# Splitting weights by whole chunks, table functions in program order, and the first norm's factor on another engine

## The chip, the cores and the metric

The kernel runs on one core of one Trainium2 chip. The metric is the device time of one execution in microseconds, as the median of several runs.

## The reference

A trunk of four layers works on 256 tokens of width 1024 in float32. Every layer is a token mixer and an MLP, each behind an RMS norm and added to the residual:

```python
for i in range(DEPTH):                       # DEPTH = 4
    kind, j = i % 3, i // 3                  # mixers a, b, c, a
    h = _rmsnorm(x, norm_mix_g[i])
    x = x + mixer[kind](h, ...)
    x = x + jnp.square(jax.nn.relu(_rmsnorm(x, norm_mlp_g[i]) @ mlp_w1[i])) @ mlp_w2[i]
return _rmsnorm(x, final_norm_g)

def _rglru_mixer(h, ...):                    # mixer a: layers 0 and 3
    gate, xr = jnp.split(h @ w_in, 2, axis=-1)          # 1024 -> 2 x 1280
    gate = jax.nn.gelu(gate)
    xr = _causal_dwconv(xr, conv_w) + conv_b            # 4 taps
    r, ig = sigmoid(block_diag(xr, gate_a_w) + gate_a_b), sigmoid(block_diag(xr, gate_x_w) + gate_x_b)
    log_a = -8 * r * softplus(-lam)
    a, u = exp(log_a), sqrt(-expm1(2 * log_a)) * (ig * xr)
    hs = scan(h_t = a_t * h_(t-1) + u_t)                # over 256 tokens
    return (hs * gate) @ w_out                          # 1280 -> 1024
```

Mixer b (layer 1) is a gated MLP whose gate is mixed over the tokens of a chunk of 128, mixer c (layer 2) a gated short convolution. The MLPs go from 1024 to 4096 and back.

## The kernel before, in words

**Layout.** Channels lie on the 128 partitions and tokens on the free axis. A tile of two channel blocks, 128x512, is a *pair*; the 1280 recurrent channels are five pairs, 0 to 4.

**Precision.** Every product is made of three float32r matmuls (`mm3`, L162, issued at L164): each operand is a high part plus a low part, and high x high, high x low and low x high are added in PSUM. The activations are split by `split` (L326: ACT casts at L329, DVE subtracts at L330) or by `prep` (L190).

**Weights.** They come as chunks of 128x2048 float32 (1 MB) in the order of their use, in two loads of 512 KB each on SP's queue (L132). ACT casts the raw half to the high part (`whi`, L135) and DVE subtracts for the low part (`wlo`, L136). The raw halves have twelve slots of 128x1024 (`rawp`, L94), the split chunks five buffers each (L95, L96). `next_chunk` (L143) keeps four split chunks ahead of the one in use. The gate weights of mixer a are block-diagonal and used whole in float32, without a split (`whole`, L114): three chunks for each of two groups, held in raw slots until TensorE has read them. A chunk's load is issued once its slot is free: after the split of the earlier tenant, or after the gate matmuls that read it.

**Order.** TensorE (PE) runs in program order (L76). The other engines' order is set by the scheduler when the kernel is built, by priorities: the weight work is put 150 places later than it stands (`LATER`), the recurrence and the norm's factor 100 earlier (`SOON`). Each engine then runs its instructions strictly in that written order.

**Mixer a** (L404 to L518) runs by `LRU_ORDER`: the convolved branch in three products (4, 2 and 4 channel blocks; weight chunks 0 and 1, 2, and 3 and 4), the gelu gate of pairs 0 and 1 (chunks 5 and 6), the first group of gate matmuls (L451; 20 instructions), the recurrence of pairs 0 and 1, the second group, the recurrence of pairs 2, 3 and 4, the gelu gate of pair 2 (one chunk) and of pairs 3 and 4 (two), then the out-projection, one chunk of 48 matmuls a pair. A pair's out-projection needs `hs` times gate (L498) as high and low part.

**The recurrence** (`recur`, L457) makes of a pair: two tanh and two exp on ACT (L467), four ops on DVE (L469 to L473), a square root on ACT (L475), then on DVE L476, L477, the affine step `q = -0.5 q - 1` (L478) and two scans (L481). ACT holds one set of table functions at a time; tanh and exp, gelu, and sqrt each call for a table load where the set changes.

**The norm.** The squares' sum goes through PE (`first`, L242, into L245), a factor 1/sqrt by ACT (L228) and 14 small ops on POOL (L229 to L235, L251, L252), DVE builds two diagonal matrices (L257), and PE spreads the factor over the partitions (`second`, L260, L263); ACT copies it out (L267). `hooks` (L502) says behind which matmuls PE does either: in layer 0 the first behind the first branch product, the second in the third.

## Time and profile before

| | |
|---|---|
| median of 3 runs | 1093.49 us (1093.09 to 1093.8) |
| the profiled execution | 1093.35 us, its span 1091.6 us |
| mean granted TensorE clock | 0.993 |
| busy: PE, DVE, ACT, POOL | 98%, 67%, 56%, 3% |
| matmuls | 9078 |
| HBM read | 202.51 MB, 186 GB/s over the span |
| table loads on ACT | 19, of 1.28 us |

Busy shares are means over stages that have different limits, so the stages are read one by one. A row of the timeline gives start, duration, engine, line, operation, output and inputs, and the number of instructions merged into it; a bracket at its end gives the idle time before it and what ended that. A row of a window gives the stretch, its length, the busy time and number of instructions of PE, of its weight loads (PEld), of DVE, ACT and POOL, then the granted clock of PE, the DMA share and GB/s. A row of a group gives the count, then busy time and mean ns of one.

### The profile page before, as it was taken

The page shows a single profiled execution, that of the slowest core. Times are in us where ns is not written, and L with a number is a line of the kernel's source. Part 1 is how long each engine was busy: PE and PEld are TensorE (multiplying, and loading weights), DVE is VectorE, ACT ScalarE, POOL GpSimd, SP SyncE. Part 2 cuts the span into 40 slices and gives each one's busy share as a digit, 9 for nine tenths or more (in the row PEclk, how much of TensorE's full clock was granted, in tenths as well). Part 3 has the DMA queues.
Part 4 walks back from the last instruction along what each step waited for, and adds up shares of the span by engine and source line. Part 5 has one row for each costly group of instructions (what it writes and reads, how often), then busy time and mean ns, then how long its engine had stood idle before and what let it go on. Part 6 is the DMA issues. An engine that isn't in the chain of part 4 may idle for free.

```text
span 1091.6 us, 21721 instructions
## 1 busy us (share of the span) xinstructions
PE 1066.9 (98%) x9078; PEld 1055.7 (97%) x9078; DVE 734.8 (67%) x991; ACT 609.7 (56%) x847; POOL 36.1 (3%) x139
## 2 busy tenths in 40 slices
PE   7998999999999999999999999999999999999996
PEld 7997999999999999999999999999999989999995
DVE  6989866555748766555777775556579698655553
ACT  6699655444655555444644555445457896544442
POOL 1000100000020100000010010000010001000000
PEclk9998999999999999999999999999999999999998
DMA  9754765555466565555466466555545447555301
GB/s 329 265 210 135 246 230 189 197 194 195 159 208 207 182 211 192 195 193 194 157 211 208 159 219 204 195 194 190 197 151 198 155 133 249 202 199 195 124 1 39
DMA packets 58802, 204.97 MB, mean 188 GB/s; under 512 B 6480, under 2 KB 8656, under 8 KB 58704
## 3 DMA queue, kind: packets, MB, share of 16 engines
q1 hardware_dynamic: 58288, 203.19, 55.0%
q8 instruction: 71, 1.16, 0.4%
q10 hardware_dynamic: 416, 0.39, 0.1%
q14 instruction: 27, 0.22, 0.1%
HBM read 202.51 MB, written 1.05 MB: 186 GB/s over the span
## 4 chain that ended last, share of the span: by engine, by line
PE 84%; DVE 7%; ACT 5%; DMA 2%; issue 1%; POOL 1%; SPq 0%; DVEq 0%; ACTq 0%; POOLq 0%
PE ps L164 80%; DMA raw<-weights 2%; PE ps L542 2%; DVE wlo L136 2%; DVE xc L481 1%; ACT q L467 1%; PE ps L451 1%; DVE xc L429 1%; ACT th L467 1%; ACT whi L135 1%; DVE ig L477 1%; ACT rg L455 0%; ACT L475 0%; ACT ig L455 0%; POOL rc L229 0%
## 5 line engine op out<-in xcount | busy, mean ns | idle before, releaser
L136 DVE TENSOR_TENSOR wlo<-raw,whi 128x1024 fp32r<-128x1024 f32 (+1 forms) x376 | 443.6, 1211 | 225.9 <-ACT whi L135 225.9
L135 ACT CAST whi<-raw 128x1024 fp32r<-128x1024 f32 (+1 forms) x376 | 376.1, 1038 | 325.2 <-issue 290.9
L164 PE MATMUL ps<-xs,whi 128*128 128x256 f32 x3200 | 550.7, 277 | 6.6 <-ACT whi L135 6.5
L164 PEld LDWEIGHTS ps<-xs,whi 128*128 128x128 f32 x3200 | 484.4, 188 | 7.0 <-ACT whi L135 6.5
L164 PE MATMUL ps<-xs,wlo 128*128 128x256 f32 x1600 | 442.9, 277 | 0.0
L164 PE MATMUL ps<-hi,whi 128*128 128x256 f32 x1312 | 363.7, 277 | 4.6 <-ACT hi L329 4.6
L164 PE MATMUL ps<-lo,whi 128*128 128x256 f32 x1312 | 364.1, 278 | 1.8 <-DVE lo L330 1.6
L164 PE MATMUL ps<-hi,wlo 128*128 128x256 f32 x1312 | 363.5, 277 | 0.7 <-DVE wlo L136 0.7
L164 PEld LDWEIGHTS ps<-xs,wlo 128*128 128x128 f32 x1600 | 301.3, 188 | 0.2 <-DVE wlo L136 0.2
L164 PEld LDWEIGHTS ps<-hi,whi 128*128 128x128 f32 x1312 | 247.6, 189 | 4.8 <-ACT hi L329 4.8
L164 PEld LDWEIGHTS ps<-lo,whi 128*128 128x128 f32 x1312 | 247.5, 189 | 2.9 <-DVE lo L330 2.5
L164 PEld LDWEIGHTS ps<-hi,wlo 128*128 128x128 f32 x1312 | 247.6, 189 | 0.9 <-DVE wlo L136 0.9
L344 DVE SCALAR_TENSOR_TENSOR u<-ps,rs 128x512 f32<-128x512 f32 x64 | 44.0, 687 | 33.2 <-PE ps L164 33.2
L346 ACT ACTIVATE hi<-u 128x512 fp32r<-128x512 f32 x64 | 40.3, 630 | 35.1 <-DVE u L344 35.1
L348 DVE TENSOR_TENSOR lo<-hsq,hi 128x512 fp32r<-128x512 f32 x64 | 44.1, 689 | 14.8 <-ACT hsq L347 12.2
L195 ACT ACTIVATE xs<-x,cst 128x256 fp32r<-128x256 f32 x64 | 29.4, 501 | 30.2 <-DVE x L315 29.1
L347 ACT ACTIVATE hsq<-u 128x512 f32<-128x512 f32 x64 | 39.4, 615 | 0.0
L196 DVE SCALAR_TENSOR_TENSOR xs<-x,cst,xs 128x256 fp32r<-128x256 f32 x64 | 28.8, 482 | 8.7 <-ACT xs L195 8.7
L229 POOL TENSOR_SCALAR rc<-rc 128x2 int32<-128x2 int32 x9 | 9.9, 1096 | 723.4 <-ACT rc L228 723.4
L257 DVE TENSOR_SCALAR diag<-eye,rc 128x128 fp32r<-128x128 f32 x36 | 8.1, 286 | 30.9 <-POOL rc L251 30.9
L451 PE MATMUL ps<-xc,raw 128*128 128x256 f32 x112 | 28.4, 379 | 0.0
L429 DVE SCALAR_TENSOR_TENSOR xc<-xr,cst,xc 128x255 f32<-128x255 f32 (+2 forms) x60 | 25.4, 481 | 0.8 <-ACT xc L425 0.6
(111 smaller groups left out, 476.0 us busy)
## 6 DMA issues: line engine op xcount, KB each, us to landing
raw<-weights SPq DMA_DIRECT2D x377, 512.0 KB, 4.7
raw<-weights SPq DMA_DIRECT2D x12, 256.0 KB, 4.5
x<-xT SPq DMA_DIRECT2D x8, 128.0 KB, 4.3
sb<-sbias SPq DMA_DIRECT2D x2, 256.0 KB, 4.9
outT<-o SPq DMA_DIRECT2D x2, 256.0 KB, 2.3
outT<-o ACTq DMA_DIRECT2D x1, 256.0 KB, 2.3
cst<-consts SPq DMA_DIRECT2D x1, 132.0 KB, 2.2
outT<-o ACTq DMA_DIRECT2D x1, 128.0 KB, 1.8
```

The source lines that it names most:

```text
L135: nc.scalar.copy(out=hi[:, s], in_=raw[:, e])
L136: nc.vector.tensor_tensor(out=lo[:, s], in0=raw[:, e], in1=hi.bitcast(F32)[:, s], op=SUB)
L164: nc.tensor.matmul(ps, a, b, start=start and n == 0, stop=stop and n == 2, skip_group_check=True)
L195: nc.scalar.activation(xs[:, hi], x, AF.Copy, scale=g)
L196: nc.vector.scalar_tensor_tensor(out=xs[:, lo], in0=x, scalar=g, in1=xs.bitcast(F32)[:, hi], op0=MULT, op1=SUB)
L344: nc.vector.scalar_tensor_tensor(out=u, in0=ps, scalar=0.0, in1=both(scale.row), op0=MAX, op1=MULT)
L346: nc.scalar.activation(hi, u, AF.Square)
L347: nc.scalar.activation(sq, u, AF.Square)
L348: nc.vector.tensor_tensor(out=lo, in0=sq, in1=hi.bitcast(F32), op=SUB)
L429: nc.vector.scalar_tensor_tensor(out=conv[:, j, d:], in0=raw[:, j, :T - d], scalar=tap(i), in1=conv[:, j, d:], op0=MULT, op1=ADD)
L451: nc.tensor.matmul(ps[:, e, :], w[:, at % 8, :], x, start=n == 0, stop=n == 1)
L467: nc.scalar.activation(dst[:, j, :], rg[i][:, j, :], fn, scale=lam[:, c:c + 1], bias=lam[:, c:c + 1])
```

## The change

Four edits. A raw slot is now a whole chunk (six slots of 128x2048 in the place of twelve of 128x1024), and a chunk is cast by one instruction and split by one, after both of its loads; chunks 0 and 1 are still done by 512 columns, and 2 and 3 by 1024 (`AHEAD` is 4). The half-width gate chunks take a whole slot each. In mixer a the table functions are chained in program order by a dependence without a semaphore (`function`), and the square roots of all pairs of a call come ahead of the DVE ops behind them. The affine step moves from DVE to ACT. In layer 0 the norm's factor is made on DVE, and its `second` moves into the second branch product; the start-up computation of `lam2` and `lam4` moves behind the first sums.

```diff
-    rawp = pool("rawp", 12 * 4096, 0, bufs=12)
+    rawp = pool("rawp", 6 * CHUNK * 4, 0, bufs=6)
...
-    def fetch(i, step=1024):
+    def fetch(i, step=CHUNK):
         n = widths[i]
         if i in whole:
-            raw = rawp.tile([P, 1024], F32, name="raw", tag="raw")
+            raw = rawp.tile([P, CHUNK], F32, name="raw", tag="raw")[:, :CHUNK // 2]
...
+        raw = rawp.tile([P, CHUNK], F32, name="raw", tag="raw")
+
+        def load(s):
+            for c in range(s.start, s.stop, 1024):
+                e = slice(c, min(c + 1024, s.stop))
+                nc.sync.dma_start(out=raw[:, e], in_=weights[i, :, e])
+
+        def part(s):
+            nc.scalar.copy(out=hi[:, s], in_=raw[:, s])
+            nc.vector.tensor_tensor(out=lo[:, s], in0=raw[:, s], in1=hi.bitcast(F32)[:, s], op=SUB)
+
+        return [(lambda s=s: load(s), lambda s=s: part(s))
+                for s in (slice(c, min(c + step, n)) for c in range(0, n, step))]
...
-                for load, part in fetch(asked[0]):
+                for load, part in fetch(asked[0], 1024 if asked[0] < AHEAD else CHUNK):
...
-    def rsqrt(ss, table=False):
+    def rsqrt(ss, table=False, eng=nc.gpsimd):
...
-        nc.gpsimd.tensor_scalar(out=y.bitcast(I32), in0=v.bitcast(I32), scalar1=-0.5, scalar2=float(RSQRT_SEED),
+        eng.tensor_scalar(out=y.bitcast(I32), in0=v.bitcast(I32), scalar1=-0.5, scalar2=float(RSQRT_SEED),
...
+    last_fn = []
+
+    def function(*args, **kw):
+        ins = nc.scalar.activation(*args, **kw).ins
+        if last_fn:
+            tc.add_manual_dep(ins, last_fn.pop().name,
+                              mybir.DependencyInfo(mybir.DependencyClass.NoSync, mybir.DependencyReason.DATA),
+                              reason="tables")
+        last_fn.append(ins)
...
             for i in pairs:
-                nc.scalar.activation(th[i], th[i], AF.Sqrt)
+                function(th[i], th[i], AF.Sqrt)
+            for i in pairs:
...
-                nc.vector.tensor_scalar(out=qs[i], in0=qs[i], scalar1=-0.5, scalar2=-1.0, op0=MULT, op1=ADD)
+                nc.scalar.activation(qs[i], qs[i], AF.Copy, scale=-0.5, bias=-1.0)
...
-        hooks = [{7: scale.first}, {}, {0: scale.second}] if layer == 0 else [{6: scale.first}, {6: scale.second}, {}]
+        hooks = ([{7: lambda: scale.first(eng=nc.vector)}, {5: scale.second}, {}] if layer == 0 else
+                 [{6: scale.first}, {6: scale.second}, {}])
...
-    softplus_lambda()
     for k in range(KD):
...
         sumsq(i)
+    softplus_lambda()
```

The tanh and exp of the gates and of the recurrence and the gelu of `gated` go through `function` too; that edit is left out above.

**What it moves.** The order in which the instructions are written, engine by engine, is shown at three places. Line numbers are each kernel's own: the cast is L135 before and L132 now, the split L136 and L133, the loads L132 (gate weights L116) and L129 (L116).

DVE, layer 0, the first weights behind chunks 0 and 1. Before, `whi_238` is chunk 2 (of raw halves 240 and 241), `whi_248` chunk 3:

```order
L136 TENSOR_TENSOR wlo_239<-raw_240,whi_238 128x1024
L136 TENSOR_TENSOR wlo_239<-raw_241,whi_238 128x1024
L136 TENSOR_TENSOR wlo_249<-raw_250,whi_248 128x1024
L257 TENSOR_SCALAR diag_398<-eye_101,rc2_394 128x128 x2
L257 TENSOR_SCALAR diag_401<-eye_101,rc2_395 128x128 x2
L136 TENSOR_TENSOR wlo_249<-raw_251,whi_248 128x1024
L136 TENSOR_TENSOR wlo_259<-raw_260,whi_258 128x1024
```

Now, behind the first halves of chunk 2 (`whi_236`) and chunk 3 (`whi_245`), from the end of the norm's factor on (`whi_254` is chunk 4, `whi_309` chunk 5):

```order
L248 CAST rc2_384<-rc_368 128x2
L249 TENSOR_TENSOR rc2_385<-rc_368,rc2_384 128x2
L254 TENSOR_SCALAR diag_388<-eye_101,rc2_384 128x128 x2
L254 TENSOR_SCALAR diag_391<-eye_101,rc2_385 128x128 x2
L133 TENSOR_TENSOR wlo_255<-raw_256,whi_254 128x2048
L133 TENSOR_TENSOR wlo_246<-raw_247,whi_245 128x1024
L133 TENSOR_TENSOR wlo_237<-raw_238,whi_236 128x1024
L133 TENSOR_TENSOR wlo_310<-raw_311,whi_309 128x2048
```

The second half of chunk 2 (`wlo_237`) has moved behind the factor, all of chunk 4 and the second half of chunk 3; SP's loads and ACT's casts of these stand in the same new order.

SP's queue, layer 0, around the loads of the gate weights (L116), with the semaphores that each waits for. Before:

```order
L116 DMA raw_423<-weights 128x1024 [waits DMAHW7_49,DVE_49]
L116 DMA raw_425<-weights 128x512 [waits DMAHW0_49,DVE_49]
L132 DMA raw_479<-weights 128x1024 [waits DMAHW1_49,DVE_49]
L132 DMA raw_480<-weights 128x1024 [waits DMAHW2_49,DVE_49]
L132 DMA raw_542<-weights 128x1024 [waits DMAHW3_49,DVE_49]
L132 DMA raw_543<-weights 128x1024 [waits DMAHW4_49,DVE_49]
```

Now:

```order
L116 DMA raw_410<-weights 128x1024 [waits DMAHW7_49,DMAHW0_49,DVE_49]
L129 DMA raw_397<-weights 128x1024
L116 DMA raw_412<-weights 128x512 [waits DMAHW7_49,DMAHW1_49,DVE_49]
L129 DMA raw_511<-weights 128x1024 [waits DMAHW2_49,PE_49]
L129 DMA raw_511<-weights 128x1024
L129 DMA raw_566<-weights 128x1024 [waits DMAHW3_49,PE_49]
L129 DMA raw_566<-weights 128x1024 [waits DMAHW4_49]
```

The chunks behind the gate weights (479 and 542 before, 511 and 566 now) waited for DVE's splits; now they wait for PE, which has to have read the gate weights in their slots.

DVE, layer 0, in the recurrence of pairs 0 and 1, from L477 (now L484) on. Before:

```order
L477 TENSOR_TENSOR ig_232<-ig_232,th_834 128x512
L481 SCALAR_TENSOR_TENSOR xc_600<-q_825,ig_231 128x256 x2
L478 TENSOR_SCALAR q_835<-q_835 128x512
L473 SCALAR_TENSOR_TENSOR ig_233<-ig_233,xc_627 128x512
L481 SCALAR_TENSOR_TENSOR xc_613<-q_835,ig_232 128x256 x2
L498 TENSOR_TENSOR xc_600<-xc_600,gate_783 128x512
L498 TENSOR_TENSOR xc_613<-xc_613,gate_786 128x512
L136 TENSOR_TENSOR wlo_726<-raw_728,whi_725 128x1024
L330 TENSOR_TENSOR lo_858<-xc_600,hi_857 128x512
L136 TENSOR_TENSOR wlo_951<-raw_952,whi_950 128x1024
L330 TENSOR_TENSOR lo_863<-xc_613,hi_862 128x512
L136 TENSOR_TENSOR wlo_951<-raw_953,whi_950 128x1024
```

Now:

```order
L484 TENSOR_TENSOR ig_230<-ig_230,th_809 128x512
L133 TENSOR_TENSOR wlo_565<-raw_566,whi_564 128x2048
L488 SCALAR_TENSOR_TENSOR xc_469<-q_800,ig_229 128x256 x2
L488 SCALAR_TENSOR_TENSOR xc_482<-q_810,ig_230 128x256 x2
L479 SCALAR_TENSOR_TENSOR ig_231<-ig_231,xc_496 128x512
L505 TENSOR_TENSOR xc_469<-xc_469,gate_758 128x512
L505 TENSOR_TENSOR xc_482<-xc_482,gate_761 128x512
L133 TENSOR_TENSOR wlo_649<-raw_650,whi_648 128x2048
L327 TENSOR_TENSOR lo_833<-xc_469,hi_832 128x512
L133 TENSOR_TENSOR wlo_704<-raw_705,whi_703 128x2048
L327 TENSOR_TENSOR lo_838<-xc_482,hi_837 128x512
L133 TENSOR_TENSOR wlo_926<-raw_927,whi_925 128x2048
```

The affine step (L478) is gone from DVE, and the splits in the stretch are others: three of the twelve rows before are splits of half a chunk, four of the twelve now are splits of a whole one. Two more whole splits (`wlo_991` and `wlo_1046`) follow ahead of the low part of pair 2 (`lo_985`).

More of the change, by code (lines that the diff above doesn't have):

```diff
@@ L123, in fetch @@
         ready[i] = (hi, lo)
-        steps = []
-        for c0 in range(0, n, 1024):
-            c1 = min(c0 + 1024, n)
-            raw = rawp.tile([P, 1024], F32, name="raw", tag="raw")
-            for c in range(c0, c1, step):
-                steps.append((raw, slice(c - c0, min(c + step, c1) - c0), slice(c, min(c + step, c1))))
-        def load(raw, e, s):
-            nc.sync.dma_start(out=raw[:, e], in_=weights[i, :, s])
-        def part(raw, e, s):
-            nc.scalar.copy(out=hi[:, s], in_=raw[:, e])
-            nc.vector.tensor_tensor(out=lo[:, s], in0=raw[:, e], in1=hi.bitcast(F32)[:, s], op=SUB)
-        return [(lambda a=a: load(*a), lambda a=a: part(*a)) for a in steps]
+        raw = rawp.tile([P, CHUNK], F32, name="raw", tag="raw")
[8 more added lines that the diff above has]
+                for s in (slice(c, min(c + step, n)) for c in range(0, n, step))]
     masked = {}
@@ L489, in gated @@
                 nc.vector.tensor_tensor(out=gate, in0=ps, in1=both(scale.row), op=MULT)
-                nc.scalar.activation(gate, gate, AF.Gelu_apprx_tanh)
+                function(gate, gate, AF.Gelu_apprx_tanh)
                 gs.append(gate)
@@ L677, in trunk @@
     scale = Scales()
-    scale.first(table=True)
+    scale.first(table=True, eng=nc.vector)
     xg = []
```

19 lines of the change are left out of this document (8 added, 11 removed).

## The prediction

> **What bounds the kernel now.** I read the page's totals first, then busy time by stretch, then the PE timeline at the stretches where PE is not full.
>
> ```profile
> PE 1066.9 (98%) x9078; PEld 1055.7 (97%) x9078; DVE 734.8 (67%) x991; ACT 609.7 (56%) x847; POOL 36.1 (3%) x139
> 65.00:92.00 27.00, 27.00 (x239) 26.97 (x238) 26.13 (x41) 25.61 (x43) 0.00 (x0) 1.00 0.53 184
> 92.00:106.00 14.00, 9.25 (x54) 8.76 (x53) 13.92 (x22) 13.16 (x15) 0.00 (x0) 0.76 0.21 69
> 338.00:839.00 501.00, 501.00 (x4419) 501.00 (x4419) 333.58 (x422) 258.06 (x339) 11.68 (x60) 1.00 0.58 192
> 883.00:904.00 21.00, 18.59 (x155) 17.85 (x154) 21.00 (x27) 17.46 (x23) 0.00 (x0) 1.00 0.67 222
> ```
>
> TensorE sets the end nearly everywhere; the long middle has no gap at all. The exceptions are the two recurrent layers: there DVE (13.92 of 14, 21.00 of 21) is the full engine, and PE waits. The size of that wait:
>
> ```profile
> 92.28 0.28 PE L164 MATMUL ps<-hi,wlo 128*128 128x256 f32 x1
> 97.17 0.58 PE L164 MATMUL ps<-hi,whi 128*128 128x256 f32 x1 [4.61 <-ACT hi L329]
> 106.34 0.39 PE L164 MATMUL ps<-lo,whi 128*128 128x256 f32 x1
> 891.93 0.39 PE L164 MATMUL ps<-lo,whi 128*128 128x256 f32 x1 [1.58 <-DVE lo L330]
> 96.00:97.00 1.00, 0.00 (x0) 0.00 (x0) 1.00 (x2) 0.50 (x1) 0.00 (x0) 0.86 0.00 0
> 97.00:98.00 1.00, 0.69 (x2) 0.40 (x2) 0.92 (x3) 1.00 (x3) 0.00 (x0) 0.50 0.00 0
> 103.00:104.00 1.00, 1.00 (x8) 1.00 (x8) 1.00 (x2) 1.00 (x2) 0.00 (x0) 0.73 0.93 262
> 134.71 158.01 PE ps L164 x1392
> 838.99 8.65 PE ps L451 x40
> ```
>
> The first four rows are PE's timeline: in layer 0 it runs out at 92.4, waits 4.6 us for the third pair of `hs` tiles, and starts its fourth pair at 106.34; layer 3 reaches the same point at 891.93. The three window rows (the clock stands third from the end) show that the wait also halves the clock, from about 96.7 to 103.5. The two chain rows give prices: 158.01/1392 = 0.1135 us a matmul at full clock, so 48 of them (one chunk) are 5.45 us; a group of gate matmuls takes 8.65. At half clock (97.9 to 103.6) some 27 matmuls ran where 53 would have: 2.9 us lost for one such wait.
>
> **The change part by part.** First the prices of a whole-chunk split, which no row has.
>
> ```profile
> L136 DVE TENSOR_TENSOR wlo<-raw,whi 128x1024 fp32r<-128x1024 f32 x368 | 438.1, 1223 | 224.0 <-ACT whi L135 224.0
> L136 DVE TENSOR_TENSOR wlo<-raw,whi 128x512 fp32r<-128x512 f32 x8 | 5.5, 685 | 1.9 <-ACT whi L135 1.9
> L135 ACT CAST whi<-raw 128x1024 fp32r<-128x1024 f32 x368 | 371.3, 1047 | 322.0 <-issue 290.9 <-ACT hsq L347 16.7 <-PE ps L164 7.2
> L135 ACT CAST whi<-raw 128x512 fp32r<-128x512 f32 x8 | 4.9, 608 | 3.2 <-DMA raw<-weights 3.2
> 76.58 1.22 DVE L136 TENSOR_TENSOR wlo<-raw,whi 128x1024 fp32r<-128x1024 f32 x1
> 77.72 0.68 DVE L330 TENSOR_TENSOR lo<-xc,hi 128x512 fp32r<-128x512 f32 x1
> ```
>
> 512 more columns cost DVE 0.538 us and ACT 0.439, so 2048 columns last 2.30 and 1.93 us (estimates by that slope). The last two rows show the next instruction starting 1.14 after a 1.22 one, so a whole split holds DVE 2.2, two halves 2.28. The saving is 0.06 to 0.08 us a chunk, some 13 us over 180 chunks, almost all of it where DVE idles; what stands behind a split now waits up to 2.2 instead of 1.14. [...]
>
> *Early stage.* The written order now puts the second half of chunk 2 behind all of chunk 4 and the second half of chunk 3, and behind the norm's factor. PE needs it as third chunk:
>
> ```profile
> 20.32 0.36 PE L164 MATMUL ps<-xs,whi 128*128 128x256 f32 x1
> 18.62 3.61 DVE L136 TENSOR_TENSOR wlo<-raw,whi 128x1024 fp32r<-128x1024 f32 x3
> 25.89 0.91 DVE L257 TENSOR_SCALAR diag<-eye,rc 128x128 fp32r<-128x128 f32 x4 [3.66 <-POOL rc L251]
> 23.62 1.05 ACT L135 CAST whi<-raw 128x1024 fp32r<-128x1024 f32 x1 [0.19 <-DMA raw<-weights]
> 1083.03 0.16 DVE L224 SCALAR_TENSOR_TENSOR rc<-rc 128x2 f32<-128x2 f32 x1
> 1083.23 0.16 DVE L225 TENSOR_TENSOR rc<-rc 128x2 f32<-128x2 f32 x1
> ```
>
> PE starts chunk 2 at 20.32 and needs the low part of its second half 26 matmuls later, at 23.3. DVE starts chunk 2's first half at 18.62 as before; then come small `sp` ops (0.5), chunk 3's first half (with the other, 2 x 1.13), the factor (a chain of 16 small ops, each 0.20 behind the one before, as in the last two rows: 3.1), the four `diag` (0.83), chunk 4 whole (2.2), chunk 3's and chunk 2's second halves (1.13 and 1.21): 11.2 us, ending 29.9. Landings (sixth in line, 23.6) and casts are earlier. So PE loses 6.6 us, of which 4.4 in one piece, and I add the 2.9 of a half clock: 9.5. The factor itself is no gain: it is ready at about 25.5 instead of 26.7, but PE passes the `second` hook only after this wait. Bounds: 6.6 without the clock, 9.5 with it.
>
> *Gates to the third pair.* The six slots of raw weights are now all held by gate weights, so SP's load of the next chunk waits for PE to finish the first gate tile (before, for a split long done), and that chunk's cast stands on ACT ahead of the last gate function:
>
> ```profile
> L451 PE MATMUL ps<-xc,raw x112: 377/379/379, 47.9 to 855.9; 128*128 128x256 f32 x112
> raw<-weights SPq DMA_DIRECT2D x377, 512.0 KB, 4.7
> DMA to landing us min/median/max: 3.0/4.6/11.0
> 61.89 1.11 ACT L467 ACTIVATE th<-rg,lam 128x256 f32<-128x256 f32 x2
> 68.70 1.16 ACT L475 ACTIVATE th<-th 128x512 f32<-128x512 f32 x2
> 69.36 1.29 DVE L476 SCALAR_TENSOR_TENSOR th<-q,th 128x512 f32<-128x512 f32 x2
> 71.18 0.42 DVE L478 TENSOR_SCALAR q<-q 128x512 f32<-128x512 f32 x1
> 71.51 0.68 DVE L477 TENSOR_TENSOR ig<-ig,th 128x512 f32<-128x512 f32 x1
> 72.11 1.26 DVE L481 TENSOR_TENSOR_SCAN xc<-q,ig 128x256 f32<-128x256 f32 x2
> 73.30 0.40 DVE L478 TENSOR_SCALAR q<-q 128x512 f32<-128x512 f32 x1
> ```
>
> Let G be the start of the gate matmuls: 47.9 before. The chunk's load is issued at G+3.5 (8 of the 20 gate matmuls), its second half lands by the 4.7 row at G+8.3, the cast ends at G+10.2, two gate functions (0.72) follow, then the chain from 61.89 to 69.36, 7.5 us with its two table loads: DVE's recurrence starts at G+18.4. From there the written order keeps DVE without a gap up to the low part of pair 2: 25 full-width ops of 0.60 (71.51 to 72.11), 10 scans of 0.595, 3 one-input ops of 0.33 (71.18 to 71.51), some 0.6 of dependence gaps, the last op 0.69, and six whole splits of 2.2: 36.4 us. Before, five halves stood in that stretch. The affine step's move to ACT takes 3 x 0.33 out, the ordering of the table functions saves six table loads of 1.3 over the whole program by the written order; neither shortens the queue named here by as much as one split. Pair 2 is complete at G+54.8, while PE arrives at 2 x 8.65 + 5 x 5.45 = G+44.6. PE waits 10 us, the clock halves (2.9), and pair 3 starts at G + 54.8 + 5.3 + 2.9 = G+63.0.
>
> Layer 0: G = 47.9 + 9.5 = 57.4, pair 3 at 120.4 against 106.34: **+14.1**. The early wait counts here only because DVE's queue hangs on G. Layer 3: G = 838.99 (the chain row), pair 3 at 902.0 against 891.93: **+10.1**. Bounds: with landings of 3.0 (the quickest raw load) and no half clock, 4.6 less each; with halves' price, 2.28, 0.5 more.
>
> *The MLPs.* Their first hidden pair hangs on a short chain behind one split:
>
> ```profile
> L344 DVE SCALAR_TENSOR_TENSOR u<-ps,rs 128x512 f32<-128x512 f32 x64 | 44.0, 687 | 33.2 <-PE ps L164 33.2
> L346 ACT ACTIVATE hi<-u 128x512 fp32r<-128x512 f32 x64 | 40.3, 630 | 35.1 <-DVE u L344 35.1
> L347 ACT ACTIVATE hsq<-u 128x512 f32<-128x512 f32 x64 | 39.4, 615 | 0.0
> L348 DVE TENSOR_TENSOR lo<-hsq,hi 128x512 fp32r<-128x512 f32 x64 | 44.1, 689 | 14.8 <-ACT hsq L347 12.2
> ```
>
> A chunk's buffer comes free 48 matmuls and two small ones (about 5.8 us) ahead of the first use of `lo`. Now a cast and split of 1.93 + 2.30 run first, then 0.69 + 0.63 + 0.52 + 0.69, with handoffs 6.9: PE waits about 1.1 in each of four layers, **+4.4** (bounds 0 and 8). Likewise whole splits stand before the last two sums of squares after each recurrent layer: **+3** (0 and 4.4, one split each); and before the last `lo` of the gating mixer: **+1** (0 and 2.2). Loads keep pace: 1.05 MB per 5.45 us is 193 GB/s, as now.
>
> Sum: 14.1 + 10.1 + 4.4 + 3 + 1 = 32.6. The profiled execution took 1093.35 us (span 1091.6, 1.75 around it), 0.14 under the median; 1093.35 + 32.6 = **1126 us**.
>
> [...]
>
> **The rivals.**
> *Full clock, shorter queue.* None of the three waits halves the clock (the early one is broken by two matmuls, the others by one), loads land at 3.0, small waits vanish: 1126 - 8.7 - 2 x 1.7 - 6 = 1108. For it: the wait of 1.58 at 891.93 shows no half clock. Against: these waits have pieces of 4 us and more. 18%.
> *Faster.* DVE is the full engine in the recurrences, and loses work there. If the splits of the gated chunks come before the recurrence, pair 2 comes before PE, and the losses go: 92.00:106.00 has 4.75 idle and 2.9 of clock, layer 3 2.4 idle; with the affine step, 1093.4 - 10 = 1083. It decides once DVE ends pair 2 before G+44.6, 10 us sooner than I find; the written order has six splits of 13.2 us ahead. 4%.
> *No change.* Only the early wait is real, 9.5, and the recurrences' 10 come back: 1093. It needs the same reversal of DVE's queue. 3%.
> *Much slower.* Splits twice as long also starve the MLPs, six slots being three chunks of loads ahead: 0.1 us in each of 180 chunks adds 18: 1144. Against it: DVE has a third of 338:839 free. 8%.
>
> **How the numbers follow.** My forecast, with 67%, covers 1114 to 1136; the low rival reaches 1108. So the range is 1110 to 1137. A measurement tells changes over 0.2% from none, 2.2 us: faster 5%, within 3%, slower 92%.
>
> **What would show it.** The changed profile should have a wait of PE on DVE's `wlo` at about 23 to 30 us, a wait of some 10 us (two pieces, on `hi` and `lo`) in each recurrent layer about 45 us after its gates start, a clock of 0.5 after each, and short waits on `lo` in all MLPs. Wrong it would be if PE is full from 20 to 60, or if DVE idles in the 36 us after the first L483.

## The result, and the profile after

The changed kernel takes 1123.7 us (median of four runs, 1122.37 to 1125.11) against 1093.63 us before: 30.1 us slower, a ratio of 1.0276 with a 95% interval of 1.0263 to 1.0289. The forecast was 1126.

First the busy line of the changed kernel's page.

```profile
PE 1073.9 (96%) x9078; PEld 1061.0 (95%) x9078; DVE 722.9 (64%) x814; ACT 588.5 (52%) x669; POOL 27.3 (2%) x124
```

DVE has 177 instructions and 12 us of work less than before, and the kernel is 30 us slower: over the whole span DVE is not what is short. Then three stretches of it by window (columns as before: PE, PEld, DVE, ACT, POOL, granted clock, DMA share, GB/s).

```profile
104.00:114.00 10.00, 1.61 (x7) 1.20 (x6) 10.00 (x15) 9.06 (x9) 0.00 (x0) 0.71 0.14 40
338.00:839.00 501.00, 499.28 (x4397) 498.76 (x4396) 317.25 (x310) 242.43 (x237) 16.08 (x73) 1.00 0.56 186
904.00:914.00 10.00, 1.76 (x12) 1.27 (x10) 10.00 (x15) 9.57 (x9) 0.00 (x0) 0.81 0.05 11
```

In the two stretches of ten microseconds, one in each recurrent layer, DVE has not a moment free and PE does next to nothing. The long middle lost 1.72 of 501 us.

PE's timeline of the changed kernel, at the places of the prediction's terms:

```profile
25.84 0.50 PE L162 MATMUL ps<-xs,whi 128*128 128x256 f32 x2 [2.03 <-ACT whi L132]
30.48 0.58 PE L162 MATMUL ps<-xs,wlo 128*128 128x256 f32 x1 [4.13 <-DVE wlo L133]
57.90 0.81 PE L459 MATMUL ps<-xc,raw 128*128 128x256 f32 x3
...
109.21 0.58 PE L162 MATMUL ps<-hi,whi 128*128 128x256 f32 x1 [5.09 <-ACT hi L326]
113.09 0.58 PE L162 MATMUL ps<-lo,whi 128*128 128x256 f32 x1 [3.30 <-DVE lo L327]
121.13 0.28 PE L162 MATMUL ps<-lo,whi 128*128 128x256 f32 x1
143.48 0.58 PE L243 MATMUL ps<-ones,sum 128*128 128x2 f32 x4 [1.23 <-DVE sum L213]
157.74 0.38 PE L162 MATMUL ps<-lo,whi 128*128 128x256 f32 x1 [0.86 <-DVE lo L345]
...
859.04 1.67 PE L459 MATMUL ps<-xc,raw 128*128 128x256 f32 x7
910.30 0.58 PE L162 MATMUL ps<-hi,whi 128*128 128x256 f32 x1 [5.12 <-ACT hi L326]
914.17 0.58 PE L162 MATMUL ps<-lo,whi 128*128 128x256 f32 x1 [3.29 <-DVE lo L327]
921.11 0.28 PE L162 MATMUL ps<-lo,whi 128*128 128x256 f32 x1
```

The early wait stands at 23.8 to 30.5. The gate matmuls start at G = 57.90 in place of 47.91. In both recurrent layers PE waits twice for pair 2, for `hi` and then for `lo`. The rows at 121.13 and 921.11 are the second matmul of pair 3, which stood at 106.34 and 891.93 before.

The new instructions by group (count, then busy time and mean ns of one):

```profile
L133 DVE TENSOR_TENSOR wlo<-raw,whi 128x2048 fp32r<-128x2048 f32 x182 | 417.0, 2291 | 250.1 <-ACT whi L132 250.0
L132 ACT CAST whi<-raw 128x2048 fp32r<-128x2048 f32 x182 | 346.7, 1907 | 306.0 <-PE ps L162 218.8 <-issue 75.0 <-DMA raw<-weights 9.2
```

A whole split is 2.29 us and a whole cast 1.91. And DVE's own timeline, from the first root product of layer 0 to the low part of pair 2 (a few of its rows; a row with x2 is two instructions):

```profile
76.63 1.29 DVE L483 SCALAR_TENSOR_TENSOR th<-q,th 128x512 f32<-128x512 f32 x2
79.04 2.29 DVE L133 TENSOR_TENSOR wlo<-raw,whi 128x2048 fp32r<-128x2048 f32 x1
...
93.79 2.29 DVE L133 TENSOR_TENSOR wlo<-raw,whi 128x2048 fp32r<-128x2048 f32 x1
...
108.98 2.29 DVE L133 TENSOR_TENSOR wlo<-raw,whi 128x2048 fp32r<-128x2048 f32 x1
111.18 1.27 DVE L488 TENSOR_TENSOR_SCAN xc<-q,ig 128x256 f32<-128x256 f32 x2
112.36 0.67 DVE L327 TENSOR_TENSOR lo<-xc,hi 128x512 fp32r<-128x512 f32 x1
```

From 76.63 to 113.03 no row has idle time ahead of it: a queue of 36.4 us, with six whole splits in it (79.04, 85.38, 88.18, 90.98, 93.79 and 108.98).

### The profile page after: what moved, and what is told of

The parts are those of the page before. It is cut to its first block, busy times and chain, and to the rows that moved or that the text cites. A ratio compares the mean times of both kernels' runs of the same rounds, so it can differ in the third digit from the quotient of the medians.

```text
span 1122.4 us, 21219 instructions
## 1 busy us (share of the span) xinstructions
PE 1073.9 (96%) x9078; PEld 1061.0 (95%) x9078; DVE 722.9 (64%) x814; ACT 588.5 (52%) x669; POOL 27.3 (2%) x124
## 4 chain that ended last, share of the span: by engine, by line
PE 83%; DVE 8%; DMA 3%; ACT 3%; issue 2%; SPq 0%; DVEq 0%; ACTq 0%
PE ps L162 78%; DMA raw<-weights 3%; DVE wlo L133 3%; PE ps L550 2%; PE ps L459 2%; ACT whi L132 1%; DVE xc L488 1%; DVE th L483 0%; DVE rg L477 0%; DVE xc L505 0%; DVE q L478 0%; DVE xs L194 0%; PE ps L586 0%; PE ps L243 0%; DVE ig L484 0%
## 5 line engine op out<-in xcount | busy, mean ns | idle before, releaser
L133 DVE TENSOR_TENSOR wlo<-raw,whi 128x2048 fp32r<-128x2048 f32 (+2 forms) x194 | 427.1, 2203 | 252.8 <-ACT whi L132 252.8
L132 ACT CAST whi<-raw 128x2048 fp32r<-128x2048 f32 (+2 forms) x194 | 355.6, 1836 | 310.8 <-PE ps L162 218.8
L162 PE MATMUL ps<-hi,whi 128*128 128x256 f32 x1312 | 364.8, 278 | 10.2 <-ACT hi L326 10.2
L193 ACT ACTIVATE xs<-x,cst 128x256 fp32r<-128x256 f32 x64 | 29.4, 502 | 30.4 <-DVE x L312 29.4
L254 DVE TENSOR_SCALAR diag<-eye,rc 128x128 fp32r<-128x128 f32 x36 | 8.1, 285 | 29.4 <-POOL rc L248 29.4
L459 PEld LDWEIGHTS ps<-xc,raw 128*128 128x128 f32 x112 | 21.1, 190 | 2.8
```

Source lines behind the costliest of these rows:

```text
L132: nc.scalar.copy(out=hi[:, s], in_=raw[:, s])
L133: nc.vector.tensor_tensor(out=lo[:, s], in0=raw[:, s], in1=hi.bitcast(F32)[:, s], op=SUB)
L162: nc.tensor.matmul(ps, a, b, start=start and n == 0, stop=stop and n == 2, skip_group_check=True)
L193: nc.scalar.activation(xs[:, hi], x, AF.Copy, scale=g)
L459: nc.tensor.matmul(ps[:, e, :], w[:, at % 8, :], x, start=n == 0, stop=n == 1)
```

## The experiments

Three theories were told apart. **A**, the prediction's: whole splits stand in DVE's written order ahead of pair 2, and their number times their length is the loss. **B**: the raw slots that the gate weights hold make the next chunk late, whatever the width of a split. **C**: the table functions in program order, with the roots grouped, delay pair 2. All ratios are against the kernel before in the same session.

### The three other edits, without whole chunks

Against the changed kernel; `fetch` with `load` and `part` is that of the kernel before.

```diff
-    rawp = pool("rawp", 6 * CHUNK * 4, 0, bufs=6)
+    rawp = pool("rawp", 12 * 4096, 0, bufs=12)
...
```

> The change without its first edit: weights in half chunks as before (twelve slots, split by 1024 columns); the table functions in program order, the affine step on ACT and the norm's factor on DVE stay. Theory A (the whole-chunk split is the loss): the time is that of before, 1093.6 us, within -3 and +4; the +4 would be PE waiting at the earlier `second` for a factor that is ready at about 25.5 us while PE passes the hook 36 matmuls after 20.3, at 24.4. Theory B (the slots held by the gate weights are the loss): the same, 1093.6. Theory C (the functions in program order and the grouped square roots delay pair 2, since its DVE ops now stand behind those of pairs 3 and 4): at least half of the recurrent layers' 24 us stays, 1105 or more.

Measured: 1098.75 us, ratio 1.0045 (1.003 to 1.006). So 25 of the 30 us are gone with the whole chunks, as A and B say, and C in its strong form falls. The rest, 5.1 us, is more than the bound given. It begins at one place, seen on PE's and on DVE's timeline of this run:

```profile
30.27 0.97 PE L262 MATMUL ps<-diag,ones_r 128*128 128x256 f32 x2 [6.13 <-DVE diag L256]
```

```profile
22.99 0.16 DVE L232 TENSOR_TENSOR rc<-rc 128x2 f32<-128x2 f32 x1
23.19 0.16 DVE L233 TENSOR_TENSOR rc<-rc 128x2 f32<-128x2 f32 x1
23.27 1.23 DVE L136 TENSOR_TENSOR wlo<-raw,whi 128x1024 fp32r<-128x1024 f32 x1
24.41 0.16 DVE L234 TENSOR_SCALAR rc<-rc 128x2 f32<-128x2 f32 x1
...
29.74 0.87 DVE L256 TENSOR_SCALAR diag<-eye,rc 128x128 fp32r<-128x128 f32 x4
```

The factor is a chain of 15 short ops (the prediction counts 16, the description of the kernel before 14), 0.20 us from one to the next. In this order a half split stands behind every third of them, so the chain, which lasts 3.0 us in the changed kernel, runs from 22.8 to 29.8, and PE, whose `second` is now in the second branch product, waits 6.1 us. The gate matmuls start at 55.7 in place of 47.9; layer 0 then makes up a part of that. In the changed kernel's order no split stands inside the chain.

### Whole chunks alone

Against the kernel before; `rawp` and `fetch` with `load` and `part` are those of the change.

```diff
-                for load, part in fetch(asked[0]):
+                for load, part in fetch(asked[0], 1024 if asked[0] < AHEAD else CHUNK):
```

> The kernel before with the first edit alone: six whole-chunk slots, casts and splits of 2048 columns; the functions, the affine step and the factor as before. Theories A and B: the whole loss is here, 1123.7 us within 4. Theory C: the loss of the recurrent layers is mostly gone, 1093.6 + 9.7 for the early wait + 3.4 for the four waits in the MLPs, 1107.

Measured: 1135.86 us, ratio 1.0385 (1.0369 to 1.04): 42.2 us slower, worse than the whole change. Theory A gave the place but not the size. PE's waits for pair 2 in the two recurrent layers:

```profile
115.76 0.58 PE L162 MATMUL ps<-hi,whi 128*128 128x256 f32 x1 [12.20 <-ACT hi L327]
922.14 0.58 PE L162 MATMUL ps<-hi,whi 128*128 128x256 f32 x1 [11.35 <-ACT hi L327]
```

DVE's queue from the first root product to pair 2's low part holds eight whole splits here and lasts 42.1 us, against six and 36.4. So the three other edits, which together cost 5.1 us on half chunks, gain 12.2 us on whole ones.

### Whole slots, half splits

```diff
-                for load, part in fetch(asked[0], 1024 if asked[0] < AHEAD else CHUNK):
+                for load, part in fetch(asked[0], 1024):
```

> The changed kernel with six whole-chunk slots, but each chunk cast and split in two halves of 1024 columns, each after its own load: slots and splits are taken apart. Theory A (width of a split and its place in DVE's written order): with halves only as much split work stands ahead of pair 2 as before, so the recurrent layers lose about 13 us in all as before (8.5 and 4.5) and the MLPs' four waits of 0.86 us go: 1093.6 to 1100. Theory B (slots): the late load behind the gate weights stays, and with it most of the 24 us: 1113 or more.

Measured: 1109.87 us, ratio 1.0149 (1.0132 to 1.0166), between the two bounds, and neither theory is enough alone. The waits in the recurrent layers are no longer for `hs` but for a weight chunk itself; PE's rows of layer 0 (layer 3 has 2.97 and 2.14 us at the same place), and the ACT row they wait for:

```profile
101.86 0.45 PE L162 MATMUL ps<-hi,whi 128*128 128x256 f32 x1 [2.97 <-ACT whi L132]
104.79 0.58 PE L162 MATMUL ps<-hi,wlo 128*128 128x256 f32 x1 [2.27 <-DVE wlo L133]
```

```profile
100.24 0.63 ACT L404 ACTIVATE gate<-gate 128x512 f32<-128x512 f32 x1
100.78 1.03 ACT L132 CAST whi<-raw 128x1024 fp32r<-128x1024 f32 x1
```

The cast at 100.78 is the first of a chunk since 85.02; ACT was busy for 14.94 of the 15 us around it (86 to 101), with the functions of the recurrence and their table loads. With whole slots the cast is written behind them.

### Gate weights in slots of their own

```diff
-    rawp = pool("rawp", 6 * CHUNK * 4, 0, bufs=6)
+    rawp = pool("rawp", 5 * CHUNK * 4, 0, bufs=5)
+    gatep = pool("gatep", 3 * CHUNK * 2, bufs=3)
...
-            raw = rawp.tile([P, CHUNK], F32, name="raw", tag="raw")[:, :CHUNK // 2]
+            raw = gatep.tile([P, CHUNK // 2], F32, name="raw", tag="graw")
...
-N_WIDE = 20
+N_WIDE = 19
```

> The changed kernel with three half-width slots for the gate weights alone and five whole-chunk slots for the rest (and 19 in the place of 20 working tiles, for the room): the load of the next chunk no longer waits for TensorE to finish a gate tile. Splits stay whole. Theory A: DVE's queue of 36.4 us ahead of pair 2's low part starts earlier by what the late cast costs ACT ahead of the last two gate functions, at most 3 us a layer; the time is 1117 to 1122. Theory B: the recurrent layers' 20 us go: 1103 or less.

Measured: 1116.14 us, ratio 1.0202 (1.0186 to 1.0217): 7.6 us less than the changed kernel, 0.9 below A's bound, far from B's. PE still waits 3.73 and 3.29 us for pair 2 in layer 0. The slots count through the order: three whole splits now stand in layer 0's queue in place of six, while its start moved from G+18.7 to G+20.0.

### The affine step alone

```diff
-                nc.vector.tensor_scalar(out=qs[i], in0=qs[i], scalar1=-0.5, scalar2=-1.0, op0=MULT, op1=ADD)
+                nc.scalar.activation(qs[i], qs[i], AF.Copy, scale=-0.5, bias=-1.0)
```

> The kernel before with the affine step alone moved from DVE to ACT. Theory A: DVE's queue ahead of pair 2's low part holds three such steps of 0.33 to 0.42 us less, so PE's wait in each recurrent layer is some 0.5 to 1 us shorter: 1092, and not slower than before. Theory D (ACT, busy 13.16 of 14 us there, becomes the bound, since a step of 128x512 lasts about 0.6 us on ACT): 1094.5 or more.

Measured: 1094.06 us, ratio 1.0005 (0.9996 to 1.0013), no change; this lies between the two bounds. The op left DVE, and the written order around it shifted: pair 2 of layer 0 is complete at G+51.3 in place of G+49.9, and PE's wait grew from 4.61 to 5.85 us. Theory A missed this: three ops less in a queue is not the same queue less three ops.

### Whole chunks and the affine step

The kernel with whole chunks alone, and this:

```diff
-                nc.vector.tensor_scalar(out=qs[i], in0=qs[i], scalar1=-0.5, scalar2=-1.0, op0=MULT, op1=ADD)
+                nc.scalar.activation(qs[i], qs[i], AF.Copy, scale=-0.5, bias=-1.0)
```

> Whole-chunk slots and splits, and the affine step on ACT; table functions and factor as before. With the chunks alone eight whole splits stand in DVE's order ahead of pair 2's low part (a queue of 42.1 us), in the changed kernel six (36.4), and the time is 1135.9 against 1123.7. Theory A-affine (the affine steps on ACT stand ahead of the casts of two chunks, whose splits so fall behind pair 2): 1118 to 1126. Theory A-functions (the table functions in program order do it): the affine step takes only some 2 us out, 1132 or more.

Measured: 1120.51 us, ratio 1.0245 (1.0231 to 1.0259). The same line that changes nothing on half chunks takes 15.4 us off here (1135.86 to 1120.51). PE's wait in layer 0 falls from 12.20 to 6.64:

```profile
108.89 0.58 PE L162 MATMUL ps<-hi,whi 128*128 128x256 f32 x1 [6.64 <-ACT hi L327]
```

Five whole splits stand in DVE's queue, three fewer than with the chunks alone, and it lasts 33.7 us. Two places on ACT's timelines go with that. With the chunks alone, four casts of whole chunks begin between 80.1 and 86.2; here three do, with an affine step between the first, at 80.80, and the others, at 84.18, and one split fewer follows in the queue. And with the chunks alone three more casts begin from 102.97 on, ahead of pair 2's high part, and two of their splits stand ahead of its low part; here the next cast begins at 108.74, behind the high part. The functions in program order are not needed for that; the changed kernel, which has them and the factor as well, is 3.2 us slower than this one.

### The early wait repaired

```diff
-                for load, part in fetch(asked[0], 1024 if asked[0] < AHEAD else CHUNK):
+                for load, part in fetch(asked[0], 1024 if asked[0] <= AHEAD else CHUNK):
...
-        hooks = ([{7: lambda: scale.first(eng=nc.vector)}, {5: scale.second}, {}] if layer == 0 else
+        hooks = ([{7: lambda: scale.first(eng=nc.vector)}, {}, {0: scale.second}] if layer == 0 else
```

> The changed kernel with chunk 4 split by 1024 columns too and `second` of layer 0 back in the third branch product, so that neither chunk 2's second half nor the factor is waited for at 23 to 31 us. Splits are whole from chunk 5 on. Theory A (the recurrence's queue hangs on the start G of the gate matmuls, so the early 9.7 us pass through to the end in full): G is 48 to 50 in place of 57.9, the waits of the recurrent layers keep their size, 1113 to 1117. Theory G (layer 0's wait is set by something that does not move with G, so it grows by what was saved): 1120 or more.

Measured: 1117.87 us, ratio 1.0221 (1.0205 to 1.0236): 5.8 us less than the changed kernel, 0.9 above A's bound. G is 50.26 in place of 57.90, so 7.6 were saved there; the splits ahead of pair 2 are six as before, its low part is ready at G+55.4 (G+55.1), and PE's waits are of the same kind:

```profile
102.38 0.58 PE L162 MATMUL ps<-hi,whi 128*128 128x256 f32 x1 [7.14 <-ACT hi L326]
105.69 0.58 PE L162 MATMUL ps<-lo,whi 128*128 128x256 f32 x1 [2.74 <-DVE lo L327]
...
906.64 0.58 PE L162 MATMUL ps<-lo,whi 128*128 128x256 f32 x1 [3.30 <-DVE lo L327]
```

The saving is still 7.5 us at pair 2 of layer 3 (906.64 against 914.17). What is lost after it is the clock: in layer 3 it stayed halved for 10.2 us in this run and for 6.8 in the changed kernel (the last section shows how). Theory A holds for what reaches pair 2 of layer 3; its bound left the clock out.

### The factor alone

Against the kernel before; `rsqrt`, `first` and the place of `softplus_lambda()` are those of the change.

```diff
-        hooks = [{7: scale.first}, {}, {0: scale.second}] if layer == 0 else [{6: scale.first}, {6: scale.second}, {}]
+        hooks = ([{7: lambda: scale.first(eng=nc.vector)}, {5: scale.second}, {}] if layer == 0 else
+                 [{6: scale.first}, {6: scale.second}, {}])
...
```

> The kernel before with the fourth edit alone: the first norm's factor on DVE, its `second` in the second branch product, the start-up computation behind the first sums. In the run with the three edits PE waited 6.1 us for the factor's diagonals at 24 to 30, and the chain of 16 small ops was spread over 7 us because a split of 1.22 us stood behind every third of them. Theory A: that wait is the whole loss of the three edits, and here it is the same, less what layer 0's own wait of 4.6 us absorbs: 1097 to 1100. Theory C (the functions in program order cost something by themselves, so this edit alone is harmless): 1095 or less.

Measured: 1097.47 us, ratio 1.0033 (1.0021 to 1.0046), 3.7 us slower, as A has it.

```profile
30.16 0.97 PE L262 MATMUL ps<-diag,ones_r 128*128 128x256 f32 x2 [6.36 <-DVE diag L256]
```

G is 55.4, so 7.5 us were lost at the start and half of that came back: DVE, no longer behind, starts the recurrence of layer 0 at G+17.0 in place of G+21.5, and the wait of 4.61 with its halved clock is gone.

### The functions alone

Against the kernel before; the other table functions of the mixer go through `function` too, as in the change.

```diff
-                nc.scalar.activation(th[i], th[i], AF.Sqrt)
+                function(th[i], th[i], AF.Sqrt)
+            for i in pairs:
...
```

> The kernel before with the second edit alone: table functions in program order, the square roots of a call's pairs ahead of the DVE ops behind them. Three edits together cost 5.1 us, the factor alone 3.7, the affine step 0.3 (no change). Theory A: what is left, 1 us, is this edit: 1093 to 1096. Theory C (it delays pair 2 and hides behind the other edits): 1097 or more.

Measured: 1095.25 us, ratio 1.0014 (1.0005 to 1.0023). Within A's bounds: by 0.14% slower, less than the 0.2% that counts as a change here. What theory C names is in the trace all the same: pair 2 of layer 0 is ready at G+53.4 in place of G+49.9, PE waits 6.51 and 1.67 us for it in place of 4.61, and PE's second matmul of pair 3 starts 3.1 us later (109.41). The span is 1.9 us longer, so a part of that comes back. The changed kernel, with its functions chained the same way, has 13 table loads of 1.28 us in place of 19. Alone, the edits thus cost 42.2, 1.5 (functions, by the ratio), 0 (affine step) and 3.7 us, some 47 in all, and together 30.

### Splits on POOL

Two versions of the kernel before, in which splits leave DVE's queue. The affine step is on ACT in both; the second takes chunks 13 to 20 in the place of 15 to 18 and has the factor on DVE, with `second` as in the version of the next section.

```diff
-            nc.vector.tensor_tensor(out=lo[:, s], in0=raw[:, e], in1=hi.bitcast(F32)[:, s], op=SUB)
+            (nc.gpsimd if i in on_pool else nc.vector).tensor_tensor(out=lo[:, s], in0=raw[:, e], in1=hi.bitcast(F32)[:, s], op=SUB)
...
+    on_pool = {f + k for f in (0, n_chunks - 53) for k in range(15, 19)}
```

> The kernel before (half chunks) with the affine step on ACT, and the low parts of four weight chunks of each recurrent layer (numbers 15 to 18 of the layer: those whose splits stand in DVE's queue of the recurrence) made on POOL in the place of DVE. Theory A (the wait of PE is DVE's queue ahead of pair 2: 22 to 26 us of the recurrence's own work plus the splits that stand in it): up to five halves of 1.13 us leave the queue in layer 0, pair 2 comes 3 to 5 us sooner, the clock need not halve there: 1086 to 1091. Theory P (POOL is too slow for it, or slows DVE while it works, so that a chunk comes late): 1093.7 or more.

> As the run before, with the low parts of chunks 13 to 20 of each recurrent layer on POOL, and the first norm's factor on DVE with `second` behind the second of the third branch product's eight steps, late enough that PE does not wait for it. Theory A: 1085 to 1090, since more splits leave DVE. Theory P: 1093.7 or more, and more than with four chunks on POOL.

Measured: 1107.56 us, ratio 1.013 (1.0116 to 1.0144), with four chunks on POOL, and 1125.09 us, 1.0289 (1.0275 to 1.0303), with eight. Theory P, and the size is in the rows of the first run: POOL's group and timeline, then DVE's timeline beside it.

```profile
L136 POOL TENSOR_TENSOR wlo<-raw,whi 128x1024 fp32r<-128x1024 f32 x16 | 43.3, 2724 | 114.8 <-ACT whi L135 97.0 <-DVE xc L482 17.8
```

```profile
77.77 5.56 POOL L136 TENSOR_TENSOR wlo<-raw,whi 128x1024 fp32r<-128x1024 f32 x2 [17.77 <-DVE xc L482]
85.56 5.15 POOL L136 TENSOR_TENSOR wlo<-raw,whi 128x1024 fp32r<-128x1024 f32 x2 [2.23 <-ACT whi L135]
```

```profile
78.26 2.82 DVE L474 SCALAR_TENSOR_TENSOR ig<-ig,xc 128x512 f32<-128x512 f32 x1
81.01 3.47 DVE L499 TENSOR_TENSOR xc<-xc,gate 128x512 f32<-128x512 f32 x2
84.56 0.69 DVE L331 TENSOR_TENSOR lo<-xc,hi 128x512 fp32r<-128x512 f32 x1
86.03 2.44 DVE L331 TENSOR_TENSOR lo<-xc,hi 128x512 fp32r<-128x512 f32 x1 [0.77 <-ACT hi L330]
88.44 2.82 DVE L474 SCALAR_TENSOR_TENSOR ig<-ig,xc 128x512 f32<-128x512 f32 x1
```

A half split lasts 2.7 us on POOL, and a DVE op beside it that reads two tiles in SBUF lasts 2.82 us in place of 0.69 and ends shortly after POOL's (the one at 88.44 at 91.26, POOL's pair at 90.71). DVE's queue has no split left in layer 0 and is 32.8 us long, where it was 28.5 with five (29.4 with the affine step on ACT), and pair 2 is ready at G+58.0.

### A version that is faster than both

From what the runs show: half chunks; the affine step on ACT; the factor on DVE, but with `second` late enough not to wait for it; and the product of `hs` and gate, with its split, at the recurrence's priority.

```diff
-        hooks = [{7: scale.first}, {}, {0: scale.second}] if layer == 0 else [{6: scale.first}, {6: scale.second}, {}]
+        hooks = [{7: lambda: scale.first(eng=nc.vector)}, {}, {1: scale.second}] if layer == 0 else [{6: scale.first}, {6: scale.second}, {}]
...
                 with tc.high_priority(offset=SOON):
                     recur(arg)
-                meet()
+                    meet()
...
```

> The kernel before (half chunks, six-step splits as before) with three small edits: the affine step on ACT; the first norm's factor on DVE with `second` of layer 0 behind the second of the eight steps of the third branch product, where PE comes after the factor's 29.8 us; and the product of `hs` and gate, with its split, given the recurrence's priority. Theory A (PE's waits in the recurrent layers follow DVE's queue ahead of pair 2; none of the three puts a split there, and the factor's place no longer costs 6.4 us): PE waits at most 2 to 3 us for pair 2 in layer 0, the clock need not halve, 1088 to 1092. Theory D (the written order shifts so that the same wait comes back, as with the affine step alone): 1092.5 to 1095.

Measured: 1091.02 us, ratio 0.9976 (0.9967 to 0.9985): 2.5 us faster than the kernel before, a little over what counts as a change here, and some 32 faster than the changed one, each against the kernel before in its own session. PE's rows of it at the factor and at pair 2 of layer 0:

```profile
29.89 0.78 PE L262 MATMUL ps<-diag,ones_r 128*128 128x256 f32 x2 [1.04 <-DVE diag L256]
...
96.12 0.39 PE L164 MATMUL ps<-hi,whi 128*128 128x256 f32 x1 [1.91 <-ACT hi L328]
96.94 0.38 PE L164 MATMUL ps<-lo,whi 128*128 128x256 f32 x1 [0.43 <-DVE lo L329]
```

The wait for the factor is 1.0 in place of 6.1, that for pair 2 is 1.9 in place of 4.6, with two half splits in DVE's queue in place of five. The clock halved all the same, though for 3.4 us in place of 6.8. Which of the three small edits carries the gain was not taken apart.

## Why the prediction was right, point by point

**The queue.** The one number on which the forecast rests is DVE's queue ahead of pair 2. The table gives it for layer 0, counted from DVE's timeline of each run; G is the first gate matmul, the queue runs from the first root product to the end of pair 2's low part, and a split counts with the time it holds DVE (1.13 a half, 2.2 a whole).

| kernel | G | queue starts | splits in it | queue | less splits | pair 2 ready | time |
|---|---|---|---|---|---|---|---|
| before | 47.9 | G+21.5 | 5 halves, 5.7 | 28.5 | 22.8 | G+49.9 | 1093.6 |
| three edits | 55.7 | G+17.0 | 2 halves, 2.3 | 29.1 | 26.8 | G+46.1 | 1098.8 |
| whole slots, half splits | 55.6 | G+18.2 | 8 halves, 9.1 | 32.8 | 23.7 | G+50.9 | 1109.9 |
| gate slots | 55.7 | G+20.0 | 3 whole, 6.6 | 32.1 | 25.5 | G+52.2 | 1116.1 |
| early wait repaired | 50.3 | G+18.6 | 6 whole, 13.2 | 36.7 | 23.5 | G+55.4 | 1117.9 |
| chunks and affine step | 57.2 | G+18.7 | 5 whole, 11.1 | 33.7 | 22.7 | G+52.4 | 1120.5 |
| the change | 57.9 | G+18.7 | 6 whole, 13.3 | 36.4 | 23.1 | G+55.1 | 1123.7 |
| chunks alone | 57.1 | G+18.6 | 8 whole, 17.5 | 42.1 | 24.6 | G+60.7 | 1135.9 |

Without its splits the queue is 22.7 to 26.8 us in these kernels (where few splits stand in it, DVE also idles: 2.9 us of it with the three edits, 1.3 with the gate slots); what differs is how many splits stand in it and how long each is. The time does not follow from the queue alone: G and other waits add to it, and with whole slots and half splits PE waits for a chunk and not for pair 2. The prediction had G+18.4 for the start (18.7), 36.4 for the queue (36.4, six whole splits) and G+54.8 for its end (55.1).

**The terms**, as they were and as they came out:

| term | predicted | measured |
|---|---|---|
| early stage, at G (part of the next) | +9.5 (6.6 wait, 2.9 clock) | +10.0 (57.90 less 47.91; waits 2.03 and 4.13) |
| layer 0, to pair 3 | +14.1 | +14.8 (121.13 less 106.34) |
| layer 3, from its G to pair 3 | +10.1 | +9.0 (62.07 against 53.10, its G being 838.83 before) |
| four MLPs | +4.4 | +3.4 (four waits of 0.86) |
| sums after the recurrent layers | +3 | +2.5 (1.23 in layer 0, and 1.23 at 943.46) |
| gating mixer | +1 | 0 (the middle window lacks 1.72, two MLP waits) |
| not foreseen | 0 | +0.8 (two waits of 0.40 for pair 4) |
| sum | 32.6 | 30.5, of 30.8 between the two spans |

That the two sums come so near is in part luck. The rows below the first three are lengths of waits. By the start times of PE's matmuls, the stretch from pair 3 of layer 0 to the gates of layer 3 lost 5.4 us where its waits add up to 4.2, and what follows pair 3 of layer 3 lost 1.6 where they add up to 2.5 (a wait of 0.40 of the kernel before, at 920.76, is gone there). In the early stage the waits were 6.2 us and not 6.6, and the rest was 3.8 and not 2.9.

The clock did halve in each of the three large waits, so the rival with the full clock (1108) fell; the two matmuls that break the early wait did not prevent it. The starved MLPs (1144) fell with the middle window, where TensorE lost 1.72 of 501 us. The rivals faster and no change needed a queue without whole splits ahead of pair 2, and it has six.

**What was wrong in the working.** Five steps, none of which carried the sum:

- "Landings and casts are earlier", of the early wait: of its two pieces the first, 2.03 us, is on the cast. ACT too had all of chunk 4 ahead of chunk 2's second half.
- "Neither shortens the queue named here by as much as one split", of the affine step and the functions. The affine step shortens it by three: on ACT, with whole chunks, it takes 15.4 us off. The count of six splits was read from the changed kernel's written order, in which this was already contained, so the sum was right and the reason given for it was not. Had the edit been priced by its duration, as it was in that sentence, a forecast for the chunks alone would have been 10 us short.
- "The early wait counts here only because DVE's queue hangs on G": it does, and 7.5 of 7.6 us saved at G arrive at layer 3. In the kernel before they would not: there DVE was behind at G, and half of a loss of 7.5 us came back.
- "The factor itself is no gain": on half chunks it is a loss of 3.7 us, which the early wait for chunk 2 covers in the changed kernel.
- "2.9 us lost for one such wait", as one price for every wait: in the traces the clock changes on a fixed grid, and equal waits lost unequal times (last section). The count behind it is a little off (5.7 us at 0.1135 hold 50 matmuls, not 53), and the price is near in layer 0. In layer 3 the halved stretch ends 2.95 us after PE's last wait and the loss is an estimated 1.8 us, half of the 3.5 us of halved clock in which PE was not waiting; 2.9 less 1.8 is the size of the difference between the 10.1 predicted there and the 9.0 measured.

**How the loss divides.** From before to the change by one step at a time: the three other edits +5.1, slots of whole chunks +11.1 (1098.75 to 1109.87), splits of whole chunks +13.8 (to 1123.7). The time from G to the second matmul of pair 3, in layers 0 and 3, shows where: 52.5 and 52.5 us with the three edits, 59.3 and 59.0 with whole slots as well, 63.2 and 62.1 in the changed kernel. So the slots' loss lies in the recurrent layers, their G being the same as with the three edits (55.6 and 55.7). Of the splits' 13.8, 7.0 lie there, 2.3 at the start (G from 55.6 to 57.9), and the rest, 4.5, goes with short waits for pair 4, for sums and in the MLPs. The prediction's working had the slots only as the reason for the late start of the queue (G+18.4). What the runs show beside that is that the slots change what is written where: a cast stands behind the recurrence's functions, or a split ahead of pair 2.

**What stays open.** That a cast or split moves in the written order because its load is expected later is argued from the rows, not tried by itself. A run with the six whole splits made shorter and everything else in its place was not made: an instruction of another length is put at another place.

## What to carry to other kernels

Where one engine works through a written order, price a larger instruction by the work that stands behind it, not by its rate: here 0.07 us saved a chunk cost 14 us, half of it because 13.3 us of splits in place of 9.1 stood ahead of one result that TensorE needed, in each of two layers, the rest at the start and in short waits behind single splits. Count the large instructions between the start of a critical chain and its end in the order as it is after the change; an edit of one line that looks free, such as the affine step, moves whole instructions over that line and is worth nothing or 15 us depending on what is beside it. And leave a chain of short ops no place where a long one can stand between its links.

## What the runs showed of the hardware

**The halved clock lasts whole steps of 3.41 us.** The windows of the changed kernel in which the clock changes (the clock stands third from the end):

```profile
26.00:27.00 1.00, 0.34 (x2) 0.14 (x2) 1.00 (x1) 0.03 (x1) 0.00 (x0) 0.62 0.71 291
36.00:37.00 1.00, 1.00 (x8) 1.00 (x8) 1.00 (x4) 0.00 (x0) 0.00 (x0) 0.76 0.79 242
...
108.00:109.00 1.00, 0.00 (x0) 0.00 (x0) 1.00 (x3) 1.00 (x3) 0.00 (x0) 0.58 0.00 0
118.00:119.00 1.00, 1.00 (x9) 1.00 (x9) 1.00 (x2) 0.00 (x0) 0.00 (x0) 0.80 0.86 279
...
910.00:911.00 1.00, 0.58 (x1) 0.29 (x1) 1.00 (x2) 1.00 (x2) 0.00 (x0) 0.64 0.00 0
917.00:918.00 1.00, 1.00 (x10) 1.00 (x10) 1.00 (x2) 0.62 (x2) 0.00 (x0) 0.94 0.08 12
```

A window of one microsecond at a mean clock of 0.62, on the way from 1.0 to 0.5, holds the change 0.24 after its start. So the clock is half from 26.24 to 36.48, from 108.16 to 118.40 and from 910.28 to 917.12: 10.24, 10.24 and 6.84 us, three, three and two times 3.41. In the kernel before the stretch was 6.82 (96.72 to 103.54), in the fastest version 3.4. The start of each is on one grid as well: with a step of 3.413, a third of 10.24, 108.16 and 910.28 are 24 and 259 steps behind 26.24, and in the kernel before the drop at 1083.18 is 289 steps behind the one at 96.72. The busy time of PE, taken step by step on this grid, shows what stood ahead of the clock's return here. In layer 0 of the changed kernel PE was busy for 0.58 and 1.90 of 3.4 us in the first two halved steps, since it was still waiting, and for all of the third, 114.99 to 118.40, behind which the clock came back. In layer 3 it was busy for 0.58 us in the first and 2.95 in the second, and two were enough. In the kernel before, 2.83 us in the step from 96.72 to 100.14 were not enough, and the full step behind it was. So equal waits cost unequal times by where they fall on the grid: the waits in the two recurrent layers of the changed kernel, 8.4 us each, start 0.63 and 1.70 us ahead of the next step of the grid (PE runs out at 104.12 and 905.18), and halved the clock for 10.2 and 6.8 us. The step ahead of a drop was not always empty: from 22.82 to 26.24 PE was busy for 1.39 of 3.42 us, and the clock fell at its end.

**A split on POOL holds up DVE.** A DVE op of 0.69 us beside a POOL split of 2.7 us lasts 2.82. In the rows of that run the ops that last so long (L474, 2.82; L331, 2.44; L499, 3.47 for two) all have two inputs in SBUF. The same run has the counterpart, one row of POOL and one of DVE:

```profile
106.10 2.64 POOL L136 TENSOR_TENSOR wlo<-raw,whi 128x1024 fp32r<-128x1024 f32 x1 [15.39 <-ACT whi L135]
106.41 0.68 DVE L490 TENSOR_TENSOR gate<-ps,rs 128x512 f32<-128x512 f32 x1
```

This DVE op, in the midst of a split on POOL, has one of its two inputs in PSUM (`ps`) and lasts 0.68 us, as in the kernel before. By what POOL holds up the others, the rows do not show.
